# Where the gated values of a streaming encoder's MLP lie in SBUF: tiles of 6144 bytes in place of 5632, and halves that start 128 bytes past a multiple of 256

## The chip, the core and the metric

The kernel runs on one NeuronCore of a Trainium2 chip. The metric is the device time of one execution in microseconds; of several runs the median is taken. TensorE does the matrix products (PE in the profile, PEld its weight loads), VectorE (DVE) and ScalarE (ACT) the elementwise work, GpSimd (POOL) a little of it, and SyncE (SP) issues most DMAs.

## What is computed

One layer of a streaming encoder for 2048 prompt tokens and 64 sample tokens, in float32: a modulated RMSNorm, one input projection split between a pooling mixer and an mLSTM, an output projection with a gated residual, and then the part that the change touches, a gated MLP with a causal convolution of width 3:

```python
h2 = rmsnorm(x, g2) * (1 + sc2) + sh2
up = h2 @ w_up                                   # 1024 -> 2 * 2816
conv = b_conv + sum(w_conv[j] * upp[:, j:j + T] for j in range(3))
a, g = jnp.split(conv, 2, -1)
x = x + gt2 * ((jax.nn.silu(g) * a) @ w_down)    # 2816 -> 1024
```

A final RMSNorm follows. Every float32 operand of a product is split into a high and a low part (`float32r`), and the kernel multiplies high by high, high by low and low by high: three matmuls where the reference has one.

## The kernel before

The 2112 tokens of the MLP are worked on in three groups of 704 (`FT`), each group in two halves of 352 (`FH`). The 22 blocks of 128 hidden channels are cut into parts of 4 or 6 blocks (`PARTS`). Of a part, each block's up-projection is computed first (`Pair.products`, matmuls of line 1633). Their moving operands are the tiles `hx`, of 6144 bytes per partition. Each `hx` tile holds four runs of 352 values, 1536 bytes apart, and a run starts `HO` = 32 values (128 bytes) into its 1536 bytes.

After that come convolution, SiLU and gate, and the gated values are split into high and low parts in the tiles `av`. The down-projection reads these tiles as moving operands, in one of two ways:

- Parts of 4 blocks go through a seven-product scheme on halves of 352 (`quad_down`, matmuls of line 2125). There are nine such parts, each with 168 matmuls: 24, then 12 of line 1633 between, then 144. The text calls such a part a quad. Its tiles are held by the class `Quad`: `put` names the half that a product needs, `both` a whole row of two halves. `wide_hi` and `wide_lo` (ACT line 1858, DVE line 1861) write two halves in one instruction; `hi` and `lo` (lines 1842 and 1845) write one.
- Parts of 6 blocks read whole rows, in pieces of 448 and 256 values (matmuls of line 2271). `split_hi` and `split_lo` write these.

An `av` tile is `[P, 2, FT]`: the high part of 704 values, then the low part, 5632 bytes with no room left. There are seven (`AVB`). They also hold the sums of the down-projection's weights while those are formed (`quad_sums`). In the built program all seven `av` tiles start 160 bytes past a multiple of 256. Since 704 values are 2816 bytes, eleven times 256, both parts of a first half start at 160, and a second half, 1408 bytes on, at 32 past a multiple of 256. All `hx` tiles start at a multiple of 256, so every one of their runs starts at 128. Every block of weights in the MLP (`wt`) starts at a multiple of 256. For comparison: the moving operands of the output projection before the MLP (`mx`, matmuls of line 496) start at multiples of 256 in the first three of its four token groups, with 512 columns, and at 128 past one in the fourth, with 256 and 320 columns in turn.

The streams of PE, ACT, DVE and POOL in the MLP are in the order in which the code is written (a manual schedule). SP issues the DMAs ahead of need.

`fscr` hands out scratch rows of 2816 bytes; of `rb` (the factor of the norm spread over all partitions) and `ssum` (the sum of squares) there is one tile each. The residual rows `x0` to `x7` stand in the same pool as `av`, on both sides of it, and share its offset of 160.

Of the kernel before, what the change touches and what calls it, by code (L numbers as in the profile page):

```python
# [9 lines left out]
F32 = mybir.dt.float32  # L10
F32R = mybir.dt.float32r
AF = mybir.ActivationFunctionType
# [4 lines left out]
P = 128  # L17
# [8 lines left out]
FT = 704  # L26
FH = FT // 2
# [3 lines left out]
AVB = 7  # L31
# [16 lines left out]
HX, HO = 2 * 384, 32  # L48
# [19 lines left out]
def tile_layer(ctx: ExitStack, tc: tile.TileContext, xT, vecs, cst, rst, w_mod, w_ada, w_qkou, w_v, w_pool,  # L68
               w_out, w_up, w_down, w_quad, st_C, st_pool, yT, yS, o_pool, o_C, o_m, o_conv):
    nc = tc.nc  # L70
    act, dve, pool, pe = nc.scalar, nc.vector, nc.gpsimd, nc.tensor
# [18 lines left out]
    def m2_ps():  # L90
        return bank("m2")
# [11 lines left out]
    def scr():  # L103
        return sp.tile([P, TMAX], F32, tag="scr", name="scr")
# [170 lines left out]
    for g in range(NG):  # L275
# [9 lines left out]
        for bi, (lo, hi) in enumerate(o.blks):  # L285
            for (a, b, s) in o.segs:
                l, h = max(lo, a), min(hi, b)
# [14 lines left out]
    def halves(key, src, n):  # L302

        out = []
        for c in (0, n // 2):
            w = n // 2
            new = (key, c) not in place_of
            kept = hl_kept[place_of.setdefault((key, c), len(place_of)), :, :, :w]
            out.append((src[:, c:c + w], w, OUT, kept) if new else (kept, w, WHOLE, None))
        return out  # L310
# [49 lines left out]
    for g in range(NFG):  # L360
        held = None
        late = []
        for (f0, f1_) in PARTS[g]:
# [13 lines left out]
            for i, (n, k) in enumerate(order):  # L377
                if i == f1_ - f0 - 2:
                    stream += late
                c = f0 + k // 4 * 4  # L380
# [223 lines left out]
    RF = cp.tile([P, 6], F32, tag="RF", name="RF")  # L604
# [27 lines left out]
    def outproj(o, mix, between, behind_heads=None):  # L632
# [5 lines left out]
        for rows in [(0, 1)] + [(n,) for n in range(2, KD)]:  # L638
            xs = nx
            Ws = [Row() for _ in rows]  # L640
            pss = [[mm_ps() for _ in o.blks] for _ in rows]
            if len(rows) == 1:
                gemm(pss[0], Ws[0], mix, o, order=order, ups=(4,))
            else:
                for W, ps in zip(Ws, pss):
                    gemm(ps, W, mix, o, ks=order[:6], order=order)
                quiet.clear()
                for W, ps in zip(Ws, pss):
                    gemm(ps, W, mix, o, ks=order[6:], order=order, late=1)
                    if behind_heads:  # L650
                        behind_heads()
                        behind_heads = None
            nx = [load_x(rows[-1] + 1, o)] if rows[-1] + 1 < KD else []
            if rows[0] == 0:
                between()
            for n, x, ps in zip(rows, xs, pss):
                for (bi, pa, pb, a, b, s) in o.pieces:
                    add = now.scalar_tensor_tensor(out=x[:, a:b], in0=ps[bi][:, pa:pb], scalar=gt1(n, s), in1=x[:, a:b],
                                                   op0=ALU.mult, op1=ALU.add)
                    if rows[0] == 0:  # L660
                        row_done.append(add)
                nc.sync.dma_start(out=x2d[n, :, o.t0:o.t0 + o.T], in_=x[:, :o.T])
            if rows[0] == 0 and o.last:
                ssum = fscr("ssum")
            for n, x in zip(rows, xs):
                sq_acc(ssum, x[:, :o.T], o.T, n == 0)
# [15 lines left out]

    def fscr(dt=F32):
        if dt in ("rb", "ssum"):
            return spare[0].tile([P, FT], F32, tag=dt, name=dt)
        return spare[0].tile([P, FT], dt, tag="fscr", name="fscr", bufs=4)


    spare = []
# [89 lines left out]
    def behind_rows(d):  # L779
# [3 lines left out]
                          reason="behind_rows")  # L783

    def sums_of(xs, put, slow=False, pin=lambda d: d):

        H = FH
# [80 lines left out]
    if True:  # L868
# [144 lines left out]
        h, pb, pr0 = [], [], []  # L1013
# [475 lines left out]
        for o in groups:  # L1489
# [16 lines left out]
            if o.g == 0:  # L1506
                t = scr()
# [13 lines left out]
            for hd in range(NH):  # L1521
# [4 lines left out]
                if o.g == 0 and hd == 0:  # L1526
                    xs = rows_of(groups[1])
                    t = scr()
# [32 lines left out]
            h = hn  # L1561
# [5 lines left out]
    f2 = fctx.enter_context(tc.tile_pool(name="f2", bufs=1, side="right"))  # L1567
# [115 lines left out]
    def quad_sums(ds, lead=7):  # L1683

        for d in ds:
            for c in (0, 256):
                t = f2.tile([P, 2, FT], F32R, tag="av", name="qs", bufs=AVB)
                w = t.bitcast(F32).rearrange("p a t -> p (a t)")[:, :1024].rearrange("p (i c) -> p i c", i=4)
                nc.sync.dma_start(out=w, in_=w_quad[d, :, :, c:c + 256])
                for _ in range(lead):  # L1690
                    yield
                a11, a12, a21, a22 = (w[:, i] for i in range(4))
                dve.tensor_tensor(out=a22, in0=a21, in1=a22, op=ALU.add)
                yield
                dve.tensor_tensor(out=a21, in0=a11, in1=a21, op=ALU.subtract)
                yield
                dve.tensor_tensor(out=a11, in0=a22, in1=a11, op=ALU.subtract)
                yield
                dve.tensor_tensor(out=a12, in0=a12, in1=a11, op=ALU.subtract)
                yield  # L1700
                yield
                nc.sync.dma_start(out=dsum[d, :, :, c:c + 256], in_=w)
                yield
                yield

    def half_tile(nm):
        return f1.tile([P, FH], F32, tag=nm, name=nm)

    class Quad:

# [4 lines left out]
        def put(self, nm, m, part):  # L1715
            key, at = {"B11": (("a", m), 0), "T1": (("a", m), 1), "B21": (("b", m), 0), "B22": (("b", m), 1),
                       "T2": (("c", m), 0), "T3": (("c", m), 1), "T4": ("d", m)}[nm]
            if key not in self.tiles:
                self.tiles[key] = f2.tile([P, 2, FT], F32R, tag="av", name="av", bufs=AVB)
            return self.tiles[key][:, part, at * FH:(at + 1) * FH]  # L1720

        def both(self, nm, m, part):
            self.put(nm, m, part)
            return self.tiles["b" if nm == "B21" else "c", m][:, part, :]

    class Pair:

# [9 lines left out]
        def products(self, old):  # L1737
# [22 lines left out]
            b3 = self.b3 = take()  # L1760
            product(b3, Bo, "T1", True)
            self.s5 = half_tile("s5")
            act.activation(self.s5, b3.t[:, :FH], AF.Copy)
            rest((old, Pair.scale_a), (older, Pair.step_3))
# [90 lines left out]
            return self.quad.gated[self.m, i]  # L1855

        def wide_hi(self, nm, t):
            act.activation(self.quad.both(nm, self.m, 0), t[:, :FT], AF.Copy)

        def wide_lo(self, nm, t):  # L1860
            dve.tensor_tensor(out=self.quad.both(nm, self.m, 1), in0=t[:, :FT],
                              in1=self.quad.both(nm, self.m, 0).bitcast(F32), op=ALU.subtract)

        def step_2(self):
# [42 lines left out]
                self.lo("T4", self.blocks()[2])  # L1907

        def split_hi(self):
            self.d = self.d or f2.tile([P, 2, FT], F32R, tag="av", name="av", bufs=AVB)  # L1910
            for (a, b, s) in self.o.segs:
                act.activation(self.d[:, 0, a:b], self.tg[:, a + 2 * s:b + 2 * s], AF.Copy)
            self.av[self.i] = self.d
# [32 lines left out]
    def final(o, x3, ssum, squares):  # L1946
# [11 lines left out]
        yield  # L1958
        box = []
        yield from bcast_cols(RF, 0, FT, box, fscr)  # L1960
        yield
        yield
# [21 lines left out]
    def final_end(o, x3, sums, lo, hi):  # L1984
# [3 lines left out]
        for _ in range(YA if lo == 0 else 0):  # L1988
            yield
        ps = m2_ps()  # L1990
        rs = f2.tile([P, 5], F32, tag="rs", name="rs", bufs=1) if lo > 0 else RF
        if lo > 0:
            dve.memset(ps[:, :len(tiles)], 0.0)
            yield
# [59 lines left out]
        for (a, b) in YG:  # L2054
            if a % 2 == 0 or b - a == 2:
                t = f1.tile([P, 2, HX], F32R, tag="hx", name="y", bufs=2 * len(BN)).bitcast(F32).rearrange(
                    "p a t -> p (a t)")[:, :3 * w].rearrange("p (k t) -> p k t", t=w)
# [146 lines left out]
    for o in fgroups:  # L2204
        Bo = B[o.g]
        held = None
        for pi, part in enumerate(PARTS[o.g]):
# [4 lines left out]
            av = [None] * nf  # L2212
# [6 lines left out]
            for f in range(f0, f1_):  # L2219
                old, pair = pair, Pair(o, Bo, f, f - f0, av, quad)  # L2220
                pair.products(old)
                if o.g == 0 and f == 2:
                    bg[0].append(quad_sums(SUMS[0]))
                    bg[1].append(prepare(fgroups[1], fscr))
                if o.g == 0 and len(x3) < KD or pi == 0 and not bg[0]:
                    x3 += load_x2(o, range(len(x3), min(len(x3) + 2, KD)))
                if held is not None and nf > 2:
                    quad_down(o, held, pair, old)
                    held = None
                    if o.g == 0:  # L2230
                        bg[0].append(quad_sums(SUMS[1], 11))
                        bg[1].extend(aside)
# [94 lines left out]
            for secs in [(c,) for c in ENDS] if ends else (ENDS,):  # L2327
                sums = [(ssum, 0)]
                for n in range(NE, KD):
                    ps = [take() for _ in secs]  # L2330
                    down(ps, rows[n], range(nf), secs, ends)
                    if ends and n == KD - 1:
                        if secs[0][0] > 0:
                            drain(0)
                        bg[0].append(final_end(o, x3, sums, *secs[0]))
                        if secs[0][0] > 0:
                            tick(0)
                    down_end(n, ps, secs)
# [98 lines left out]
```

## Time and profile before

| | before |
|---|---|
| three runs | 2158.36, 2160.7, 2164.97 us (median 2160.7) |
| profiled execution: its time, its span | 2162.09 us, 2160.3 us |
| PE busy | 2142.7 us, 99% |
| DVE, ACT, POOL busy | 1650.1, 1101.7, 253.8 us |
| DMA moved | 541.09 MB, mean 250 GB/s |
| matmuls on `hx` (line 1633), on `av` halves (line 2125), on `av` rows (line 2271) | 5544, 1512, 1440 |

A matmul's recorded duration is longer than the distance to the next one's start, since matmuls overlap. In a row of the timeline, a start, a duration and a count stand side by side; the pace is the duration less that of the last matmul, over the count less one.

### The profile page before, as it was taken

The page shows a single profiled execution, that of the slowest core. Times are in us where ns is not written, and L with a number is a line of the kernel's source. Part 1 is how long each engine was busy: PE and PEld are TensorE (multiplying, and loading weights), DVE is VectorE, ACT ScalarE, POOL GpSimd, SP SyncE. Part 2 cuts the span into 40 slices and gives each one's busy share as a digit, 9 for nine tenths or more (in the row PEclk, how much of TensorE's full clock was granted, in tenths as well). Part 3 has the DMA queues.
Part 4 walks back from the last instruction along what each step waited for, and adds up shares of the span by engine and source line. Part 5 has one row for each costly group of instructions (what it writes and reads, how often), then busy time and mean ns, then how long its engine had stood idle before and what let it go on. Part 6 is the DMA issues. An engine that isn't in the chain of part 4 may idle for free.

```text
span 2160.3 us, 38129 instructions
## 1 busy us (share of the span) xinstructions
PE 2142.7 (99%) x13556; PEld 2038.7 (94%) x13556; DVE 1650.1 (76%) x3060; ACT 1101.7 (51%) x2192; POOL 253.8 (12%) x470
## 2 busy tenths in 40 slices
PE   8999999999999999999999999999999999999998
PEld 7888888888899999999999999999999999999998
DVE  5777768678675779788688668988886597887875
ACT  4554335234323557465556445655655364564554
POOL 0010000001000301010001110100101221121112
PEclk9999999999999999999999999999999999999999
DMA  8987997898799588797669986665668675455442
GB/s 321 326 315 237 317 324 246 282 320 274 243 298 302 196 280 307 252 336 246 233 219 314 329 299 207 235 214 205 228 222 273 218 261 182 171 180 183 172 169 85
DMA packets 296839, 541.09 MB, mean 250 GB/s; under 512 B 25760, under 2 KB 112800, under 8 KB 296648
## 3 DMA queue, kind: packets, MB, share of 16 engines
q1 hardware_dynamic: 286600, 514.13, 69.9%
q10 hardware_dynamic: 10048, 24.51, 2.9%
q8 instruction: 107, 1.75, 0.3%
q14 instruction: 84, 0.69, 0.1%
HBM read 412.56 MB, written 125.98 MB: 249 GB/s over the span
## 4 chain that ended last, share of the span: by engine, by line
PE 89%; DVE 5%; DMA 3%; issue 1%; ACT 1%; SPq 0%; POOL 0%; DVEq 0%; ACTq 0%; POOLq 0%
PE mm L1633 35%; PE mm L496 24%; PE mm L2271 10%; PE mm L2125 10%; PE mm L1171 3%; DVE wt L432 1%; DMA wt<-wsum 1%; PE m L1361 1%; PE m L1383 1%; PE m L1381 1%; PE m L1346 1%; DMA w<-w_ada 1%; DVE x L2094 1%; DVE tg L1611 1%; ACT tg L1606 0%
## 5 line engine op out<-in xcount | busy, mean ns | idle before, releaser
L1633 PE MATMUL mm<-hx,wt 128*128 128x352 f32 x5544 | 888.8, 321 | 2.2 <-DVE wt L432 1.3
L1633 PEld LDWEIGHTS mm<-hx,wt 128*128 128x128 f32 x5544 | 881.0, 188 | 4.5 <-DVE wt L432 3.2
L496 PE MATMUL mm<-hl,wt 128*128 128x512 f32 (+2 forms) x1920 | 385.3, 356 | 0.0
L432 DVE TENSOR_TENSOR wt<-raw,wt 128x512 fp32r<-128x512 f32 (+1 forms) x460 | 310.4, 681 | 75.0 <-ACT wt L429 74.9
L496 PEld LDWEIGHTS mm<-hl,wt 128*128 128x128 f32 x1920 | 314.8, 188 | 46.8 <-issue 3.6
L429 ACT ACTIVATE wt<-raw 128x512 fp32r<-128x512 f32 (+1 forms) x460 | 274.1, 603 | 163.3 <-PE mm L496 53.9
L2125 PE MATMUL mm<-av,wt 128*128 128x352 f32 x1512 | 247.4, 323 | 1.4 <-DVE x L2094 0.7
L2125 PEld LDWEIGHTS mm<-av,wt 128*128 128x128 f32 x1512 | 242.3, 188 | 4.0 <-DVE wt L432 2.0
L2271 PE MATMUL mm<-av,wt 128*128 128x448 f32 (+1 forms) x1440 | 231.3, 322 | 0.0
L2271 PEld LDWEIGHTS mm<-av,wt 128*128 128x128 f32 x1440 | 220.9, 188 | 9.7
L2094 DVE SCALAR_TENSOR_TENSOR x<-mm,MOD,x 128x352 f32<-128x352 f32 (+3 forms) x368 | 171.7, 507 | 73.3 <-PE mm L2271 58.3
L1681 ACT ACTIVATE mm<-mm 128x352 f32<-128x352 f32 x204 | 91.4, 448 | 240.9 <-PE mm L1633 177.1
L496 PE MATMUL mm<-mx,wt 128*128 128x512 f32 (+1 forms) x960 | 182.6, 352 | 0.0
L496 PEld LDWEIGHTS mm<-mx,wt 128*128 128x128 f32 x960 | 159.3, 188 | 22.5
L1611 DVE SCALAR_TENSOR_TENSOR ta<-ea,V,ta 128x704 f32<-128x704 f32 (+1 forms) x132 | 125.7, 952 | 61.3 <-ACT ta L1606 56.8
L1611 DVE SCALAR_TENSOR_TENSOR tg<-eg,V,tg 128x704 f32<-128x704 f32 (+1 forms) x132 | 125.7, 952 | 52.7 <-ACT tg L1606 50.2
L432 DVE TENSOR_TENSOR wt<-wt 128x512 fp32r<-128x512 f32 x204 | 138.8, 684 | 12.7 <-ACT wt L429 10.6
L429 ACT ACTIVATE wt<-wt 128x512 fp32r<-128x512 f32 x204 | 123.6, 621 | 31.3 <-DMA wt<-wsum 30.5
L1589 POOL COPY ea<-UC 128x2 f32<-128x2 f32 x66 | 34.7, 525 | 539.3 <-DVE ta L1611 425.3
L1829 ACT ACTIVATE tg<-tg 128x704 f32<-128x704 f32 (+1 forms) x66 | 52.5, 795 | 71.1 <-DVE tg L1611 71.1
L1171 PE MATMUL mm<-wt,hl 128*128 128x256 f32 (+1 forms) x576 | 71.2, 284 | 0.0
L1171 PEld LDWEIGHTS mm<-wt,hl 128*128 128x128 f32 x576 | 70.2, 189 | 0.8 <-issue 0.6
(315 smaller groups left out, 2204.4 us busy)
## 6 DMA issues: line engine op xcount, KB each, us to landing
wt<-wsplit SPq DMA_DIRECT2D x132, 512.0 KB, 4.3
raw<-w_up SPq DMA_DIRECT2D x198, 256.0 KB, 4.1
wt<-hl_kept SPq DMA_DIRECT2D x96, 512.0 KB, 6.0
wt<-wsum SPq DMA_DIRECT2D x132, 256.0 KB, 4.9
wsplit<-wt SPq DMA_DIRECT2D x66, 512.0 KB, 5.0
w<-w_up SPq DMA_DIRECT2D x88, 256.0 KB, 4.6
wsum<-w SPq DMA_DIRECT2D x44, 512.0 KB, 5.4
Bd<-fscr ACTq DMA_DIRECT2D x56, 352.0 KB, 3.9
```

The lines of the kernel that those rows point to most:

```text
L429: act.activation(u.w[:, 0, :u.n], u.raw[:, :u.n], AF.Copy)
L432: dve.tensor_tensor(out=u.w[:, 1, :u.n], in0=u.raw[:, :u.n], in1=u.w[:, 0, :u.n].bitcast(F32), op=ALU.subtract)
L496: pe.matmul(ps[bi][:, :hi - lo], U[:, a, k % 4 * P:(k % 4 + 1) * P], mv[k][:, b, lo:hi], start=(at == 0 and pi == 0), stop=(k == order[-1] ...
L1171: pe.matmul(ps[ti][:n, :cols], h[4 * kh + k4][:, b, lo:lo + n], U[:, a, k4 % 2 * cols:(k4 % 2 + 1) * cols], start=(kh == 0 and k4 == 0 and ...
L1589: pool.tensor_copy(ext[:, 0:2], UC[:, f, :])
L1611: dve.scalar_tensor_tensor(out=t[:, :E], in0=ext[:, j:j + E], scalar=wc(j, f), in1=t[:, :E], op0=ALU.mult, op1=ALU.add)
L1633: pe.matmul(bk.t[:, :FH], U[:, a, kc * P:(kc + 1) * P], Bo.at(nm, kc, b), start=(first and kc == 0 and pi == 0), stop=(kc == 3 and pi == 2 ...
L1681: act.activation(to.t[:, :FH], bk.t[:, :FH], AF.Copy)
L1829: act.activation(self.tg[:, :E], self.tg[:, :E], AF.Silu)
L2094: dve.scalar_tensor_tensor(out=x3[n][:, a:b], in0=bk.t[:, a - lo:b - lo], scalar=gt2(n, s), in1=x3[n][:, a:b], op0=ALU.mult, op1=ALU.add)
L2125: pe.matmul(bk.t[:, :FH], U[:, a, c:c + P], quad.put(op, m, b), start=(first and m == 0 and pi == 0), stop=(m == 1 and pi == 2), skip_grou ...
L2271: pe.matmul(bks[i].t[:, :hi - lo], U[:, a, k % 4 * P:(k % 4 + 1) * P], av[k][:, b, lo:hi], start=(k == 0 and (a, b) == PASSES[0]), stop=(k ...
```

## The change

An `av` tile becomes `[P, 2, HX]` with `HX` = 768: 6144 bytes, the high and the low part 3072 bytes apart. For a quad, each part is cut into two slots of 1536 bytes with a half of 352 values at the start of each. Whole rows are taken from the eighth value on (32 bytes in), without a gap between the halves. `wide_hi` and `wide_lo` now write two runs of 352 with a gap of 128 bytes in place of one run of 704; `halves` gives the source the same shape.

To make room, `ssum` takes the one tile that `rb` has, by having the same tag; 2816 bytes are freed. The tag of the small tile `rs` gets a second buffer of 32 bytes, of which nothing is written; the pool is laid out against the end of the memory, and its other tiles move by that much. In the built program all `av` tiles then start 128 past a multiple of 256: all halves, of both parts, are at 128, and whole rows are at 160 as before. `x0` to `x7` go from 160 to 128, `rb` from 128 to 0.

```diff
     def fscr(dt=F32):
         if dt in ("rb", "ssum"):
-            return spare[0].tile([P, FT], F32, tag=dt, name=dt)
+            return spare[0].tile([P, FT], F32, tag="rb", name=dt)
...
-                t = f2.tile([P, 2, FT], F32R, tag="av", name="qs", bufs=AVB)
+                t = gated("qs")
...
+    def gated(name="av"):
+        return f2.tile([P, 2, HX], F32R, tag="av", name=name, bufs=AVB)
+
+    def halves(t):
+        return t[:, :FT].rearrange("p (h t) -> p h t", h=2)
...
             if key not in self.tiles:
-                self.tiles[key] = f2.tile([P, 2, FT], F32R, tag="av", name="av", bufs=AVB)
-            return self.tiles[key][:, part, at * FH:(at + 1) * FH]
+                self.tiles[key] = gated().rearrange("p a (h t) -> p a h t", h=2)[:, :, :, :FH]
+            return self.tiles[key][:, part, at]
...
         def wide_hi(self, nm, t):
-            act.activation(self.quad.both(nm, self.m, 0), t[:, :FT], AF.Copy)
+            act.activation(self.quad.both(nm, self.m, 0), halves(t), AF.Copy)
 
         def wide_lo(self, nm, t):
-            dve.tensor_tensor(out=self.quad.both(nm, self.m, 1), in0=t[:, :FT],
+            dve.tensor_tensor(out=self.quad.both(nm, self.m, 1), in0=halves(t),
                               in1=self.quad.both(nm, self.m, 0).bitcast(F32), op=ALU.subtract)
...
-            self.d = self.d or f2.tile([P, 2, FT], F32R, tag="av", name="av", bufs=AVB)
+            self.d = self.d or gated()[:, :, 8:8 + FT]
...
-        rs = f2.tile([P, 5], F32, tag="rs", name="rs", bufs=1) if lo > 0 else RF
+        rs = f2.tile([P, 5], F32, tag="rs", name="rs", bufs=2) if lo > 0 else RF
```

No instruction is added, removed or moved: on every engine and queue the built programs have the same instructions in the same order, and each waits for the same semaphore values. What differs are addresses and, in 36 ACT and 36 DVE instructions, the shape (2 runs of 352 in place of 704).

More of the change, by code (lines that the diff above doesn't have):

```diff
@@ L1718, in put @@
             if key not in self.tiles:
-                self.tiles[key] = f2.tile([P, 2, FT], F32R, tag="av", name="av", bufs=AVB)
-            return self.tiles[key][:, part, at * FH:(at + 1) * FH]
+                self.tiles[key] = gated().rearrange("p a (h t) -> p a h t", h=2)[:, :, :, :FH]
+            return self.tiles[key][:, part, at]
         def both(self, nm, m, part):
             self.put(nm, m, part)
-            return self.tiles["b" if nm == "B21" else "c", m][:, part, :]
+            return self.tiles["b" if nm == "B21" else "c", m][:, part]
     class Pair:
```

## The prediction

> **What bounds the kernel.** I read the page first, for the engine that sets the time, then the timeline of PE alone, for the pace of each kind of matmul, and last what DVE does in the nine quads.
>
> ```profile
> span 2160.3 us, 38129 instructions
> PE 2142.7 (99%) x13556; PEld 2038.7 (94%) x13556; DVE 1650.1 (76%) x3060; ACT 1101.7 (51%) x2192; POOL 253.8 (12%) x470
> ...
> PE 89%; DVE 5%; DMA 3%; issue 1%; ACT 1%; SPq 0%; POOL 0%; DVEq 0%; ACTq 0%; POOLq 0%
> ...
> L1633 PE MATMUL mm<-hx,wt 128*128 128x352 f32 x5544 | 888.8, 321 | 2.2 <-DVE wt L432 1.3
> ...
> L2125 PE MATMUL mm<-av,wt 128*128 128x352 f32 x1512 | 247.4, 323 | 1.4 <-DVE x L2094 0.7
> ...
> L2271 PE MATMUL mm<-av,wt 128*128 128x448 f32 (+1 forms) x1440 | 231.3, 322 | 0.0
> ```
>
> PE is busy for 99% of the span and carries 89% of the chain that ended last. A change that adds and removes no instruction can gain only by the pace of matmuls, or by the few microseconds in which PE waits. The mean durations (321, 323, 322 ns) don't show the pace, because matmuls overlap. The timeline does; its columns are start, duration, engine, line, operation, count:
>
> ```profile
> 1107.87 23.21 PE L2125 MATMUL mm<-av,wt 128*128 128x352 f32 x144
> 1130.92 12.10 PE L1633 MATMUL mm<-hx,wt 128*128 128x352 f32 x74
> ...
> 1344.88 51.47 PE L1633 MATMUL mm<-hx,wt 128*128 128x352 f32 x324
> 1396.18 4.01 PE L2125 MATMUL mm<-av,wt 128*128 128x352 f32 x24
> ...
> 1658.48 42.15 PE L2271 MATMUL mm<-av,wt 128*128 128x448 f32 x264
> ```
>
> Both kinds of line 1633 and 2125 stream 352 columns against 128 by 128 weights, three passes per block. On `hx` a matmul starts every (51.47 - 0.32) / 323 = 158.36 ns; on the halves in `av` every (23.21 - 0.32) / 143 = 160.07 ns. From start to start it is the same: 1107.87 to 1130.92 is 23.05 us for 144, and 1344.88 to 1396.18 is 51.30 for 324. The difference is 1.71 ns per matmul. The runs in `hx` begin 128 bytes past a multiple of 256 and end on one; the halves in `av` begin at 160 or 32. After the change they begin and end as those in `hx` do.
>
> **The change part by part.**
>
> *Halves at 128.* If start and end set the pace, 1512 matmuls gain 1.71 ns: 2.59 us at most. Not all of it reaches the end, since two of the nine quads run at DVE's pace:
>
> ```profile
> 1482.61 8.97 PE L2125 MATMUL mm<-av,wt 128*128 128x352 f32 x54
> 1492.31 14.69 PE L2125 MATMUL mm<-av,wt 128*128 128x352 f32 x90 [0.74 <-DVE x L2094]
> ...
> 1563.89 1.45 PE L2125 MATMUL mm<-av,wt 128*128 128x352 f32 x8
> 1565.88 22.40 PE L2125 MATMUL mm<-av,wt 128*128 128x352 f32 x136 [0.53 <-DVE wt L432]
> ```
> ```profile
> core 0: us, DVE busy (x), PEclk, DMA share, GB/s
> 1107.90:1130.90 23.00, 20.04 (x38) 1.00 0.52 172
> ...
> 1482.70:1506.80 24.10, 21.98 (x42) 1.00 0.52 179
> 1563.90:1588.00 24.10, 22.50 (x44) 1.00 0.52 175
> 1773.50:1796.60 23.10, 21.23 (x52) 1.00 0.53 178
> ```
>
> In the second and third window PE stops for 0.74 and 0.53 us until DVE has added to the residual or split weights, and these quads take 24.1 us where the others take 23.0 to 23.2. What is late there is DVE, and a faster PE waits longer for it. I count their 2 x 168 matmuls as no gain (336 x 1.71 = 0.57 us). The gain then lies between 2.59 us, if these two gain too, and 2.02. I take **2.0 us**: in both the stop comes after some of the 144 matmuls, so at least what these gain is lost, and DVE is busy for over 91% of the whole of both.
>
> *Whole rows.* They start at 160 as before, and their pace, (42.15 - 0.32) / 263 = 159.05 ns over pieces of 448 and 256 columns, stays. What does change for them is the distance of low from high part, 2816 to 3072 bytes. In `hx` that distance is 1536. No row of this trace has 3072. The nearest is that 158.36 on one side and the present 159.05 on the other, so I take 0; the end below is the same 1.71 ns for 1440 matmuls, 2.5 us, the end above nothing, since no row shows a slower pace for such pieces than the present one.
>
> *Two runs in place of one (wide copies).* Here is the cost of the present instructions, and of two that write one run and four runs of 512 values:
>
> ```profile
> L1861 DVE TENSOR_TENSOR av<-tg,av 128x704 fp32r<-128x704 f32 x36 | 31.9, 885 | 0.1
> L1845 DVE TENSOR_TENSOR av<-tg,av 128x352 fp32r<-128x352 f32 x54 | 28.2, 522 | 12.1 <-ACT av L1842 12.0
> L432 DVE TENSOR_TENSOR wt<-wt 128x512 fp32r<-128x512 f32 x204 | 138.8, 684 | 12.7 <-ACT wt L429 10.6 <-DMA yT<-x 2.0
> L268 DVE TENSOR_TENSOR nd<-nd,sf 128x512 f32<-128x512 f32 x16 | 11.1, 692 | 15.1 <-POOL sf L1404 15.1
> ```
> ```profile
> L1858 ACT ACTIVATE av<-tg 128x704 fp32r<-128x704 f32 x36 | 28.2, 784 | 9.4 <-DVE tg L1837 9.3
> L1842 ACT ACTIVATE av<-tg 128x352 fp32r<-128x352 f32 x54 | 26.5, 490 | 16.4 <-DVE tg L1837 10.3 <-DVE tg L1849 6.1
> ```
>
> `nd` is written as four runs of 128 with a gap between, at 692 ns against 684 for one run: 8 ns for three more runs. So 885 becomes some 888 ns, and 36 of them cost DVE 0.1 us, which lies beside PE's work but for the two quads at DVE's pace (8 of 36: 0.02 us). The upper end is that a two-run instruction costs as much as two of one run: 2 x 522 - 885 = 159 ns on DVE and 2 x 490 - 784 = 196 ns on ACT. The lower end is 0. I take 0, by the row of `nd`, which is the one with gaps.
>
> *One tile for `rb` and `ssum`.* A shared tile can bring a wait of the one's writer for the other's last reader. The built programs wait for the same values at the same places, so there is none: 0 from both sides. The extra 32 bytes of `rs` cost nothing but address space.
>
> *Residual rows and `qs` at 128 in place of 160.* DVE reads and writes them, DMAs fill and empty them. DVE's 368 additions of line 2094 now work on halves at 160 or 32, afterwards at 128 or 0. The fills of `x` take a median of 5.8 us, those of `fscr`, whose rows start on multiples of 256, 4.8 us for the same size:
>
> ```profile
> x<-x2d SPq DMA_DIRECT2D x24, 352.0 KB, 5.8
> ...
> fscr<-x2d SPq DMA_DIRECT2D x16, 352.0 KB, 4.8
> ```
>
> Should the 1 us be the offset's, it is still hidden: the rows are loaded while the products run, and no wait of PE in this trace is for `x` from a DMA. Its cover is the 50 us of products ahead of each quad (the row of 324). I take 0; from below at most the two stops of 0.74 and 0.53 us could go, if DVE's part in them became quicker.
>
> The sum against the profiled execution: span 2160.3 - 2.0 = 2158.3 us, its time 2162.09 - 2.0 = 2160.1. That execution lies 1.4 us over the median of the three runs (2160.7), so I predict 2160.7 - 2.0 = **2158.7 us** for the median, -0.09%. A change within 0.3% (6.5 us) is about what this kernel's measurement can't tell from none.
>
> **The rivals.**
>
> *The offset is not what sets the pace: 2160.7 us.* For it speaks another tile at 128:
>
> ```profile
> 344.84 43.72 PE L496 MATMUL mm<-mx,wt 128*128 128x512 f32 x192
> 732.12 51.36 PE L496 MATMUL mm<-mx,wt 128*128 128x256 f32 x384
> ```
>
> The first row has 512 columns from multiples of 256, at (43.72 - 0.39) / 191 = 226.9 ns. The second has 256 and 320 columns in turn (288 in the mean), all from 128, at (51.36 - 0.31) / 383 = 133.3 ns. From 512 columns to the 352 of the halves it is 66.8 ns for 160 columns, 0.418 per column; from these to 288 it is 26.8 ns for 64, 0.418 too. So `mx` at 128 lies on the line of the tiles at 0, 32 and 160, and only `hx` lies 1.7 ns below it. Against the rival: these pieces of `mx` also end at 128, while those of `hx` end on a multiple of 256, as the new halves will; and 352 columns at two different offsets, 160 and 32, have one pace. The Trainium skill, page "SBUF — State Buffer", section "Door 1: The DMA port swizzle", speaks for this rival: SBUF has lines of 16 bytes, and an access pays where it crosses into a new line with too few hits in the last. 0, 32, 128 and 160 all begin such a line and every run is contiguous, so by that rule all these paces would lie on one line, and the halves would gain nothing: 2160.7 us. The trace disagrees for `hx` (158.36 against 160.07) and agrees for `mx`.
>
> *Whole rows gain as well: 2156.2 us.* If the parts' distance (a multiple of 512 bytes in `hx` and in the new tiles, not in the old ones, nor in `mx`, whose parts lie 2304 apart) is what counts, 1440 matmuls gain 1.71 ns too, 2.5 us more. For it speaks that `mx` is then explained; beyond that no row speaks for or against it, and it needs a second rule beside the one of the forecast.
>
> *Slower: the wide copies at the price of two instructions, 2171.5 us.* In a quad, `wide_hi` and `wide_lo` stand right ahead of the products that read them. At their upper ends 36 pairs cost 36 x (0.159 + 0.196) = 12.8 us, and with all of that on PE's path it would be 2158.7 + 12.8. To be slower by over 6.5 us it needs 8.5 us on the path, 0.24 us for each pair. Against it: 8 ns for three more runs in `nd`, and PE's rows of 144 without a stop in the quads outside of DVE's pace, so ACT and DVE have room.
>
> **How the numbers follow.** Halves alone gain: 0.60, 2158.7. No gain: 0.23, 2160.7. Rows gain as well: 0.09, 2156.2. Copies slower: 0.04, up to 2171.5. The other 0.04 is for a moved stop, either way. Three runs of one kernel spread over 6.6 us, so the range adds some 4 us to either side of the first and second: 2154.5 to 2163.5, which leaves out the copies, the lower part of the third case's spread, and the farther of the moved stops. Faster by over 0.3% needs 4.5 us beyond the forecast, rows and a vanished stop together or spread: 0.07. Slower by over 0.3%: 0.05, the copies mostly. Within: 0.88.
>
> **What would show it.** Right: rows of 144 of line 2125 at 22.8 us for 144 starts in place of 23.05, `hx` and the rows of 264 unchanged, wide copies at 780 to 790 and 885 to 890 ns, the quads at DVE's pace still near 24 us. Wrong: rows of 144 still at 23.05 (the first rival); rows of 264 under 41.5 us (the second); wide copies over 950 ns with PE stopping for `av` (the third). I would also be wrong if a stop of PE of over 2 us appeared at another place, since DVE's order against PE's shifts by the gain.

## The result and the profile after

| | before | changed |
|---|---|---|
| median of 16 runs each | 2160.73 us | 2178.12 us |
| lowest, highest | 2157.83, 2167.48 us | 2158.07, 2184.13 us |
| profiled execution: its time, its span | 2162.09, 2160.3 us | 2161.37, 2159.6 us |

The ratio over all runs is 1.0066, 95% interval 1.0052 to 1.0081 (that of the two medians alone is 1.0080): slower by under 1%, clear of the noise, and outside of the predicted range. The runs of the changed kernel are spread in an unusual way. Three of 16 lie between 2158.07 and 2162.07 us, the other 13 between 2172.01 and 2184.13. The profiled execution is one of the three short ones, so its page looks as if the forecast had come true. First the page, then PE's timeline (start, duration, engine, line, operation, count) at a whole quad and at a whole row:

```profile
span 2159.6 us, 38129 instructions
PE 2142.5 (99%) x13556; PEld 2037.2 (94%) x13556; DVE 1649.8 (76%) x3060; ACT 1104.0 (51%) x2192; POOL 256.2 (12%) x470
...
L1633 PE MATMUL mm<-hx,wt 128*128 128x352 f32 x5544 | 890.7, 322 | 0.7 <-DVE wt L432 0.6
...
L2131 PE MATMUL mm<-av,wt 128*128 128x352 f32 x1512 | 245.5, 322 | 2.1 <-DVE x L2100 0.7
```
```profile
1111.80 22.96 PE L2131 MATMUL mm<-av,wt 128*128 128x352 f32 x144
1134.60 5.71 PE L1633 MATMUL mm<-hx,wt 128*128 128x352 f32 x35
...
1506.27 51.46 PE L1633 MATMUL mm<-hx,wt 128*128 128x352 f32 x324
...
1657.75 42.15 PE L2277 MATMUL mm<-av,wt 128*128 128x448 f32 x264
```

The halves take 1134.60 - 1111.80 = 22.80 us for 144 starts, 158.33 ns each, as forecast; whole rows are unchanged at 42.15 us for 264. But two rows do not fit, one of them in the trace of the kernel before:

```profile
1143.31 55.93 PE L1633 MATMUL mm<-hx,wt 128*128 128x352 f32 x334 [0.29 <-DVE wt L432]
```
```profile
937.95 55.93 PE L1633 MATMUL mm<-hx,wt 128*128 128x352 f32 x334 [0.27 <-DVE wt L432]
```

The first is of before, the second of the changed kernel. Here a matmul starts every (55.93 - 0.33) / 333 = 167.0 ns, with the same operands' shapes and offsets as in the row of 324, where it is (51.46 - 0.32) / 323 = 158.33. The granted clock is 1.00 in both. So a stream of these matmuls has two paces, and the prediction read only one. A longer execution of the changed kernel (2171.49 us, from the tenth run below) shows what that is worth; its page, its timeline and a window, then the same window of the short execution:

```profile
span 2169.7 us, 38129 instructions
...
L1633 PE MATMUL mm<-hx,wt 128*128 128x352 f32 x5544 | 897.2, 323 | 0.7 <-DVE wt L432 0.6
...
L2131 PE MATMUL mm<-av,wt 128*128 128x352 f32 x1512 | 249.8, 324 | 1.8 <-DVE x L2100 0.7
```
```profile
1767.60 24.40 PE L2131 MATMUL mm<-av,wt 128*128 128x352 f32 x144
1791.84 54.16 PE L1633 MATMUL mm<-hx,wt 128*128 128x352 f32 x324
1845.84 4.16 PE L2131 MATMUL mm<-av,wt 128*128 128x352 f32 x24
1849.84 2.16 PE L1633 MATMUL mm<-hx,wt 128*128 128x352 f32 x12
1851.84 24.16 PE L2131 MATMUL mm<-av,wt 128*128 128x352 f32 x144
1875.84 54.16 PE L1633 MATMUL mm<-hx,wt 128*128 128x352 f32 x324
...
2043.84 68.16 PE L1633 MATMUL mm<-hx,wt 128*128 128x352 f32 x408
2111.84 3.45 PE L2277 MATMUL mm<-av,wt 128*128 128x448 f32 x20
```
```profile
1800.00:2100.00 300.00, 300.00 (x1801) 1.00 0.52 172
```
```profile
1800.00:2100.00 300.00, 299.79 (x1889) 1.00 0.53 176
```

From 1770 to 2110 us every row has one pace, from start to start (1845.84 - 1791.84) / 324 = 166.67 ns, products and halves alike: 2055 matmuls in one piece. In the windows (PE's busy time, its matmuls, its clock) PE is busy all the time in both; in one it starts 1801 matmuls, in the other 1889. Busy time and granted clock show nothing of it. Only a count over a stretch, or a row's duration over its count, does.

### The profile page after: what moved, and what is told of

Read it like the earlier page. It is cut to its first block, busy times and chain, and to the rows that moved or that the text cites. A ratio compares the mean times of both kernels' runs of the same rounds, so it can differ in the third digit from the quotient of the medians.

```text
span 2159.6 us, 38129 instructions
## 1 busy us (share of the span) xinstructions
PE 2142.5 (99%) x13556; PEld 2037.2 (94%) x13556; DVE 1649.8 (76%) x3060; ACT 1104.0 (51%) x2192; POOL 256.2 (12%) x470
## 4 chain that ended last, share of the span: by engine, by line
PE 88%; DVE 5%; DMA 4%; issue 2%; ACT 1%; SPq 0%; POOL 0%; DVEq 0%; POOLq 0%; ACTq 0%
PE mm L1633 36%; PE mm L496 23%; PE mm L2277 10%; PE mm L2131 9%; PE mm L1171 3%; DVE wt L432 1%; DVE x L2100 1%; PE m L1361 1%; PE m L1383 1%; DMA hl_kept<-wt 1%; PE m L1381 1%; PE m L1346 1%; DMA mx<-xT 1%; DMA wt<-wsum 1%; DVE tg L1611 0%
```

## The experiments

The theory: at 128 a stream of 352-column matmuls has two paces, 158.33 and 166.67 ns, and keeps the one that it starts in until something ends it (**L**, two paces). Its rivals: the shared tile or the moved rows bring a new wait (**W**), and the new place of the halves is slow by itself (**P**).

**The changed kernel once more, and its parts.** Four kernels, measured together. The first is the changed kernel again, run once:

> The changed kernel once more, for a trace of one of its long executions: 13 of its 16 runs took 2172 to 2184 us, and the one profiled was not among them (2161.4). Theory A (the quicker quads let DVE fall behind, and PE waits): the 17 us stand as idle time of PE, in or next to the quads, matmuls of line 2131 at 158.3 ns. Theory B (an address slows an engine or a DMA in most executions): the pace of a group of instructions or the landing time of a group of DMAs is different from the trace of the short execution, by 17 us in all, and it has to be one whose tile moved: halves (12 ns each over 1512), rows (12 ns over 1440), or x and qs. Theory C (nothing of this kernel, a state of the chip): the loss is spread over all stages, the attention ahead of the MLP too, which has no changed address.

It took 2164.62 us. Its timeline:

```profile
1313.22 4.16 PE L2131 MATMUL mm<-av,wt 128*128 128x352 f32 x24
...
1319.22 24.16 PE L2131 MATMUL mm<-av,wt 128*128 128x352 f32 x144
1343.22 54.16 PE L1633 MATMUL mm<-hx,wt 128*128 128x352 f32 x324
...
1427.22 54.16 PE L1633 MATMUL mm<-hx,wt 128*128 128x352 f32 x324
```

The quad of 144 takes 24.0 us from start to start, where that of the short execution took 22.80, and the slow pace runs on through products, quad and products: 1092 matmuls in one piece. The longest slow piece in before is the one of 334. None of the three theories of this run holds as it stands. Against A: quads run at 166.67 ns, and PE's stops in the streams of 352 columns add up to 5.8 us, less than the 7.6 of the short execution. Against B, which wanted a group whose tile moved: the products on `hx` are slow too, and their runs lie at 128 as before. Against C: from the first matmul to the first of line 1633 it takes 777.2 us in this trace, 777.7 in the short one and 777.5 in that of before.

The second moves the halves by 8 values, to 160, and leaves all else:

```diff
-... .rearrange("p a (h t) -> p a h t", h=2)[:, :, :, :FH]
+... .rearrange("p a (h t) -> p a h t", h=2)[:, :, :, 8:8 + FH]
```

> The changed kernel with each half 8 values later in its slot (160 past a multiple of 256, as the first halves before), all else as in the change. Theory A (the quicker pace of the halves upsets a wait): halves at 160.0 ns, time back to 2160 to 2162 us in all runs. Theory B (placement of x, qs, rb or the rows): still 2172 to 2184 in most runs. Theory C (state of the chip): as the kernel before in the same call or slower with it.

2165.38 us (2158.92 to 2169.47), ratio 1.0021 [1.0011, 1.0032]. That is neither A's 2160 to 2162 us in all runs nor B's 2172 to 2184. It spreads over 10.6 us where the changed kernel spreads over 26, and its highest run lies 2.5 us below the group of 13. So most of the loss hangs on the halves' place, not on the tiles' size or on the shared tile.

The third is before with only the shared tag for `rb` and `ssum`:

```diff
-            return spare[0].tile([P, FT], F32, tag=dt, name=dt)
+            return spare[0].tile([P, FT], F32, tag="rb", name=dt)
```

> The kernel before with one part of the change alone: the sum of squares in the spread factor's tile; no other address moves. Theory A: 2160 to 2162 us. Theory B, if the shared tile or rb at 0 is what costs: over 2170 in most runs; if it is x or av: 2160 to 2162.

2161.21 us, ratio 1.0002 [0.9993, 1.0012]: the sharing costs nothing, and W falls for it. The fourth is before with only the second buffer of `rs`, which moves `av`, `x` and `qs` to 128 and the halves to 128 and 0:

```diff
-        rs = f2.tile([P, 5], F32, tag="rs", name="rs", bufs=1) if lo > 0 else RF
+        rs = f2.tile([P, 5], F32, tag="rs", name="rs", bufs=2) if lo > 0 else RF
```

> The kernel before with the 32 bytes of rs alone: av, qs and x move from 160 to 128 past a multiple of 256, halves from 160 and 32 to 128 and 0, rows from 160 to 128. Theory A: first halves (half of 1512) at 158.3 to 160 ns, so 2158 to 2161 us, or long runs if any quickening upsets a wait. Theory B, if x or qs at 128 is what costs: over 2170 us in most runs.

2164.52 us, ratio 1.0018 [1.0008, 1.0027]. No run is over 2169 us, so W falls for `x` and `qs` as well, though A's 2158 to 2161 us is missed too. Its whole rows start at 128, and they alone explain most of it:

```profile
1657.57 42.68 PE L2271 MATMUL mm<-av,wt 128*128 128x448 f32 x264
```

That is (42.68 - 0.32) / 263 = 161.06 ns against 159.05 from 160, 2.0 ns for 1440 matmuls or 2.9 us.

**Can the pace be taken away, or cut?** Three kernels and a scan, measured together. The changed kernel again, for another long execution:

> The changed kernel a third time, for its spread on this chip and for one more trace. Theory L (lock): a stream of 352-column matmuls from 128 past a multiple of 256 has two steady paces, 158.3 and 166.7 ns, and keeps the one that it starts in until PE stops or a matmul from another offset comes between. In the changed kernel products and quads are one stream, so the slow pace can hold over several quads. The time is then 2156 us plus 8.33 ns for each matmul at 166.7: 2161 for 600, 2166 for 1200, 2178 for 2600. Rival W (waits): the time over 2160 is idle time of PE, and the pace is 158.3 ns throughout.

2171.80, 2183.51 and 2164.83 us; the profiled one (the first) had a slow piece of 1044 matmuls at its end. It has 2040 slow matmuls in all, for which the sum of L gives 2173 us; 2171.80 were measured. Next, 18 extra matmuls in the changed kernel, at the start of each quad and ahead of the first product behind it, of 64 columns; their result is overwritten by the matmul that follows:

```diff
         if first:
             bk.start(FH)
+            if cut:
+                cut.pop()
+                pe.matmul(bk.t[:, :64], ones_r, ones_r[:, :64], start=True, stop=True)
...
+                    if not count:
+                        pe.matmul(bk.t[:, :64], ones_r, ones_r[:, :64], start=True, stop=True)
```

> The changed kernel with 18 small matmuls more (64 columns of ones, from another offset, overwritten by what follows), one at the start of each quad and one at the first product after it. Theory L: the slow pace can't cross these places, so a stretch at 166.7 ns has at most some 400 matmuls, as in the kernel before; the runs come back to 2157 to 2166 us, median about 2161, none over 2172. If one small matmul doesn't end the slow pace, as the change itself. Rival W: 18 matmuls more change no wait, and most runs stay at 2172 to 2184.

2168.49 us (2166.14 to 2170.60), ratio 1.0034 [1.0021, 1.0047]. The right half: no slow piece is longer than the 408 of the products between two of the extra matmuls, and no run is over 2171 us. At one quad:

```profile
1508.13 0.19 PE L1634 MATMUL mm<-ones_r 128*128 128x64 f32 x1
1508.16 54.23 PE L1637 MATMUL mm<-hx,wt 128*128 128x352 f32 x324
1562.23 0.19 PE L2133 MATMUL mm<-ones_r 128*128 128x64 f32 x1
1562.26 4.04 PE L2137 MATMUL mm<-av,wt 128*128 128x352 f32 x24
```

The slow 324 end at the extra matmul, and the 24 behind it are fast. The missed half is the median: some streams start slow right behind an extra matmul, as the 324 do here.

Then before with products' tiles at 32 in place of 128 (`HX, HO = 2 * 384, 8`):

> The kernel before with the runs of hx starting 32 bytes into their slots (HO = 8) in place of 128. Theory L: at 32 past a multiple of 256 there is one pace, 160.0 ns, as the old second halves show, and no slow stretches. Of 5544 matmuls those at 158.3 lose 1.67 ns (up to 9.2 us) and those at 166.7 (324 in the trace of before, 2.7 us) gain: 2166 to 2169 us, with less spread than the kernel before (its runs 2157.5 to 2164.8). Rival (what counts is the distance of the parts, not the start): 158.3 ns and 2160 us as before.

2165.18 us (2164.11 to 2166.67), ratio 1.0015 [1.0005, 1.0025], 0.8 us below the forecast. All of `hx` runs at one pace, (52.00 - 0.32) / 323 = 160.0 ns, and the runs spread over 2.6 us, where those of before, measured beside it, spread over 10.4:

```profile
1343.65 52.00 PE L1633 MATMUL mm<-hx,wt 128*128 128x352 f32 x324
```

So the second pace goes with the place 128, and with it most of the spread. P falls: 128 is at its first pace the quicker place (158.33), and the loss lies in the second. The scan gives each tile of products in before another start (`AT = dict(B11=0, T1=4, T2=8, B21=16, B22=24, T3=28, T4=32)`, in values of 4 bytes):

> The kernel before with another start for each of the seven operands of the up-projection: B11 at 0, T1 at 16, T2 at 32, B21 at 64, B22 at 96, T3 at 112 and T4 at 128 bytes past a multiple of 256, each read by 12 matmuls in a row. Theory L in its narrow form (only 128 has two paces): T4 alone at 158.3 or 166.7, the others at 160.0. In a wider form (what counts is whether start or end meets a boundary of 64 or 128 bytes): B11 and B21 as well. By the rule of 16-byte lines all seven have one pace, as all seven starts are multiples of 16.

2169.31 us, in one run. Mean distance of starts, worked out from the trace's records over pieces of twelve without a stop, 62 to 66 pieces each:

```
start past a multiple of 256 bytes    0      16     32     64     96     112    128
ns from start to start              161.2  160.0  160.3  160.1  162.6  161.6  158.8
```

At 128 it is 158.5 in most pieces and 166.0 and 166.1 in two. No other start is as quick, and in these short pieces none shows a second pace. The narrow form of L is half right: 128 alone has two paces, but 0, 96 and 112 are not at 160.0.

**What ends the slow pace?** `T4`, one operand of each quad, goes back to where it lay before the change (160 and 32), so that twelve matmuls of another place stand between the streams:

```diff
+                self.tiles[key] = (gated()[:, :, 8:8 + FT].rearrange(...) if nm == "T4" else
```

> The changed kernel, but with the operand T4, the last of each half of a quad, where it lay before (its first half at 160, its second at 32 past a multiple of 256, without a gap); the other six at 128 as in the change. So each quad has six matmuls from 160 and 32 in its middle and six more right ahead of the products that follow... for both row blocks, 24 of its 168. Theory L: the stream from 128 is cut at the end of each half of a quad, in the way in which the kernel before cut it, so no slow stretch is longer than some 500 matmuls, and starts after 32 seldom fall to the slow pace (none of 18 in the traces of before and of the kernel that only shares the tile). 1296 matmuls keep 158.3 ns, 2.2 us less half a microsecond: median 2157.5 to 2160.5, none over 2170. If starts after 32 fall to the slow pace as often as starts after a stop (15 of 148), 2162 to 2168. Rival W (waits): as the change, 2172 to 2184.

2185.87 us (2184.42 to 2189.41), ratio 1.0115 [1.0099, 1.0132]: missed by far, the slowest of all. The changed kernel beside it, the run from which the lines of the long execution are:

> The changed kernel in the same call, for comparison and one more trace. Theory L: 2158 to 2184 us with a median over 2168; in its trace, 2155 to 2156 us plus 8.33 ns for each matmul at 166.7 ns, within 2 us. Rival W: the time over 2160 is idle time of PE.

2182.06 us (2171.49 to 2186.35), ratio 1.0081 [1.0056, 1.0107]. Its highest run is 2 us over the forecast. Its trace has 2052 slow matmuls, so L gives 2172.1 to 2173.1 us; 2171.49 were measured, while the stops of PE in these streams went down (6.4 us against 7.6 in the short execution), so the rival W falls. Then I blamed the matmul that stands last before a stream, and took extra matmuls of 256 columns from 160, a place behind which no stream had started slow so far (0 of 40, behind whole rows), at the places of the first extra ones:

```diff
-                pe.matmul(bk.t[:, :64], ones_r, ones_r[:, :64], start=True, stop=True)
+                pe.matmul(bk.t[:, :256], ones_r, quad.raw[:, 0, 8:264], start=True, stop=True)
```

> The changed kernel with 18 other matmuls more, at the same places as the 18 of 64 columns: 256 columns from 160 past a multiple of 256, the form of the last piece of a whole row; what they write is overwritten. In ten traces so far none of 40 streams that began after such a piece took the slow pace, against 17 of 178 after a stop. Theory L with the way of entry set by the last matmul before: none of the 18 streams that begin behind the new matmuls is slow, slow stretches begin at stops alone and end within 324 matmuls; 18 x 0.12 = 2.1 us more than the fast form (2154 to 2156.5 us): median 2157 to 2161, none over 2168. Theory L with the way of entry set by a longer history (the six-matmul pieces of T4 let the slow pace through): streams begin slow there as after 64 columns, some one in six or more, and the median is 2164 us or more.

2183.88 us (2176.49 to 2188.55), ratio 1.0107 [1.0091, 1.0124]: missed again, so the last matmul before a stream doesn't set its pace. Its timeline shows what happens in its place:

```profile
1343.95 0.28 PE L1633 MATMUL mm<-av,ones_r 128*128 128x256 f32 x1
1344.07 54.15 PE L1636 MATMUL mm<-hx,wt 128*128 128x352 f32 x324
1398.06 0.28 PE L2135 MATMUL mm<-av,ones_r 128*128 128x256 f32 x1
1398.17 4.15 PE L2139 MATMUL mm<-av,wt 128*128 128x352 f32 x24
...
1404.17 24.16 PE L2139 MATMUL mm<-av,wt 128*128 128x352 f32 x144
1428.16 0.28 PE L1633 MATMUL mm<-av,ones_r 128*128 128x256 f32 x1
1428.28 54.15 PE L1636 MATMUL mm<-hx,wt 128*128 128x352 f32 x324
```

The slow pace is handed on over the extra matmul, 13 times out of 13 in this trace. The last run takes the same matmuls at the same places with 64 columns of the same tile, so that only the length differs:

> The changed kernel with the 18 extra matmuls of the run before (at the start of each quad and ahead of the first product after it, reading the quad's own tile at 160), 64 columns long in place of 256. The records of the two runs with extra matmuls differ in more than the length: 64 columns of the row of ones (at 224) ended the slow pace in 5 places of 5 where a slow stream ran into one, 256 columns of the quad's tile (at 160) in none of 13. Behind the 64 columns the second matmul starts some 247 ns after the first, so PE stands still for some 90 ns; behind the 256 columns nothing stands still (280 ns over both). Theory G (the short standstill ends the slow pace): the 64 columns of the quad's tile leave the same standstill and end it in every place, no slow stretch is longer than 408 matmuls, and the median is that of the run with ones, 2166 to 2171 us. Theory T (what is read, or its place, decides): the slow pace is passed on as by the 256 columns of the same tile, stretches of over 1000 matmuls stand in the trace, and the median is 2178 to 2188 us.

2163.66 us (2161.38 to 2167.32), ratio 1.0015 [1.0005, 1.0024], 20 us below the 256 columns:

```profile
1342.12 0.19 PE L1633 MATMUL mm<-av,ones_r 128*128 128x64 f32 x1
1342.14 54.23 PE L1636 MATMUL mm<-hx,wt 128*128 128x352 f32 x324
1396.22 0.19 PE L2135 MATMUL mm<-av,ones_r 128*128 128x64 f32 x1
1396.25 4.05 PE L2139 MATMUL mm<-av,wt 128*128 128x352 f32 x24
...
1402.03 22.96 PE L2139 MATMUL mm<-av,wt 128*128 128x352 f32 x144
```

The slow 324 end at the extra matmul; the quad behind it is fast. No slow piece is longer than 333. Both kinds cost the same: from the last matmul ahead of it to the first behind, 256 columns take 280 ns in place of 158, 122 more; with 64 columns the second one behind starts 435 ns after in place of 317, 118 more. So the 20 us are not their price. That the operand's place decides falls: place and tile were the same, and the length alone made the difference. That it is the standstill behind the short matmul which ends the slow pace fits, though the time was put too high; it was not tested apart from the length.

All traces together, counted in the records of twelve executions (all but the kernel with `hx` at 32 and the scan):

```
what stands between two streams at 128            slow before: ended, handed on   fast before: next slow, next fast
24 matmuls of whole rows, from 160                    18   0                          0   37
one extra matmul of 64 columns                         8   0                          4   22
one extra matmul of 256 columns                        0  13                          2    2
12 halves at 160 and 32 (T4 moved back)                1  11                          4    2
12 halves at 0                                         2   0                          0   16
24 or 144 halves at 160 and 32, as in before           1   0                          0   33
144 halves at 160                                      3   0                          1    5
a stop of PE, a start 225 ns or more after the last    4   2                         18  127
```

## Why the prediction was wrong

**The step that failed** is the term "Halves at 128: 1512 matmuls gain 1.71 ns". It took the pace at 128 as one number, read from a row of 324. The runs showed two, 158.33 and 166.67 ns, of which the second is 8.33 ns slower than the first and 6.67 slower than the 160.0 that the halves had. The table counts slow matmuls in blocks of twelve and takes off 8.33 ns for each, and 2.1 us for the 18 extra matmuls where there are any. Then it takes off PE's stops: each step of 225 ns or more between two 352-column matmuls of these lines, less 159 ns, without the step behind an extra matmul.

| execution | its time | slow matmuls | time without them | stops | time without both |
|---|---|---|---|---|---|
| before | 2162.09 | 324 | 2159.4 | 8.3 | 2151.1 |
| before, shared tile | 2159.43 | 240 | 2157.4 | 7.0 | 2150.4 |
| changed, halves at 160 | 2160.23 | 444 | 2156.5 | 6.3 | 2150.3 |
| changed, short | 2161.37 | 588 | 2156.5 | 7.6 | 2148.9 |
| changed, three others | 2164.62, 2171.80, 2171.49 | 1272, 2040, 2052 | 2154.0, 2154.8, 2154.4 | 5.8, 6.6, 6.4 | 2148.2, 2148.2, 2148.0 |
| changed, extra 64 columns (ones; quad's tile) | 2170.19, 2163.31 | 1548, 900 | 2155.2, 2153.7 | 7.1, 5.3 | 2148.1, 2148.4 |
| changed, extra 256 columns | 2185.72 | 4008 | 2150.2 | 2.5 | 2147.7 |
| changed, T4 moved back | 2184.42 | 3852 | 2152.3 | 3.6 | 2148.7 |

The times differ by 26 us. Without both, the eight executions with halves at 128 (in the last, all but those of T4) lie within 1.2 us of each other, and the three with halves at 160 or 32 some 2 us above them. So the gain of the faster halves is there and about as large as the term said (2.59 us at most). But the 2040 slow matmuls of the longest traced execution of the changed kernel cost 17.0 us, of which the fewer stops give some back. No execution of the changed kernel over 2172 us was traced. By the same sum a time of 2184 us would take some 3400 to 4000 slow matmuls (an estimate); the two last rows show that a kernel of this build gets to as many.

**A second misreading, a small one.** The prediction counted seven quads as free of DVE. From start to start, the 144 matmuls of the nine quads took 23.05, 23.06, 23.42, 24.23, 24.22 and four times 23.32 us in before, and 22.80, 22.85, 23.22, 24.32, 24.11, 23.22, 23.21, 23.22 and 23.20 in the short execution, where no half was slow. Only the first two gained most or all of the 0.25 us that 144 halves should. The last four stop for 0.27 us in before and for some 0.34 in the short execution, and gained 0.10 to 0.12. All 1512 halves together took 1.2 us less, where 2.0 were forecast. What the last four wait for is seen in the weight loads (PEld), which the forecast does not show: one line of before, then two of the short execution:

```profile
1774.81 3.35 PEld L2125 LDWEIGHTS mm<-av,wt 128*128 128x128 f32 x21 [0.29 <-DVE wt L432]
```
```profile
1854.21 0.69 DVE L432 TENSOR_TENSOR wt<-wt 128x512 fp32r<-128x512 f32 x1
...
1854.95 1.10 PEld L2131 LDWEIGHTS mm<-av,wt 128*128 128x128 f32 x7 [0.36 <-DVE wt L432]
```

DVE finishes the low part of a weight block at 1854.90 us, and the load of that block starts at 1854.95. A faster PE only waits longer there, as the prediction said of the two quads that it did see.

**Why more are slow after the change.** In before, halves at 160 and 32 stand between the streams of products. They have one pace, 160.0 ns, and no stream behind them was slow (0 of 34, of which one came behind a slow stream; 144 halves at 160 ended three more of three). In the changed kernel products and quads are one stream, so a start that happens to be slow lasts through several quads. The slow pace seems to protect itself, too. Two rows of the short execution at one of the last four quads:

```profile
1853.46 23.37 PE L2131 MATMUL mm<-av,wt 128*128 128x352 f32 x144
1876.66 51.46 PE L1633 MATMUL mm<-hx,wt 128*128 128x352 f32 x324
```

The 144 take 0.41 us more than the 22.96 of the whole quad above: this is the stop for DVE's weight block, some 1.1 us into each of these four quads, and the stream starts anew behind it. The execution of 2171.49 us has this stop in the first of the four alone (24.40 in place of 24.16); the stream that starts behind it is the slow one. From there on PE is late enough to stop no more (no weight load in these quads waits for DVE), and nothing ends the stream before the whole rows. The execution of 2171.80 us does the same two quads later: a stop in the first three, a slow stream behind the third, no stop in the fourth. That the slow pace keeps itself up in this way is read from these two traces; no run tests it.

**Right** were: the fast pace of the halves (22.80 us for 144); the two quads at DVE's pace, still at 24.32 and 24.11 us; whole rows at 42.15 us for 264, so the rival of rows that gain falls; `rb` and `ssum` in one tile at 0; residual rows and `qs` at 128 with no new wait of PE for them; and the wide copies, forecast at 780 to 790 and 885 to 890 ns:

```profile
L1867 DVE TENSOR_TENSOR av<-tg,av 128x704 fp32r<-128x704 f32 x36 | 32.0, 888 | 0.1
```
```profile
L1864 ACT ACTIVATE av<-tg 128x704 fp32r<-128x704 f32 x36 | 28.3, 785 | 8.6 <-DVE tg L1843 8.4
```

So the rival of slow copies falls as well. That the short execution lies within the predicted range is luck: 588 of its matmuls were slow, and nothing in the runs holds the number there. The rival that the offset does not set the pace falls by the run with `hx` at 32 (158.33 to 160.0). The rule that the Trainium skill has in "SBUF — State Buffer", section "Door 1: The DMA port swizzle", would give all starts of the scan one pace, since each is a multiple of 16 bytes; the trace disagrees, with 158.8 to 162.6 ns.

**The range** came from the spread of three runs of before, which was itself for the most part the two paces: with `hx` at 32, ten runs spread over 2.6 us. None of the rivals held a second pace, and the row that shows it (334 matmuls, 55.93 us) stood in the trace of before, next to the one of 74 that I quoted.

**Open** is what decides the pace at a start: 18 of 145 streams started slow behind a stop and a fast stream, with nothing in the records to tell them apart. Open too is why the two kinds of extra 64 columns differ by some 5 us in the median, why the halves at 160 stay 0.2% above before, and why 24 matmuls of whole rows end the slow pace without a standstill (18 of 18) where twelve halves do not, or why a stop of PE ends it only 4 times of 6. No version that was run is faster than before.

## What to carry to other kernels

Before a pace is taken as a price, work it out for every long row of the timeline, not for one, and look for a second value at full clock: here the spread between executions was for the most part such a second value. Read the weight loads for waits as well as the matmuls. An operand at an offset that is slower by 1% may be what ends a bad pace (here four slow streams of four), so a change that makes all operands alike can lengthen what was short before. And where runs of one kernel fall into two groups, one profiled execution says little until it is known to which group it belongs.

## What the runs showed of the hardware

- 352-column matmuls with a weight load each, at a granted clock of 1.00, have two steady paces when the moving operand starts at 128 past a multiple of 256 bytes: 158.33 and 166.67 ns, kept for as many as 2055 matmuls.
- At starts of 32 and 160 the pace is 160.0 ns in long rows. In pieces of twelve, 16, 32 and 64 have 160.0 to 160.3 ns, and 0, 96 and 112 have 161.2, 162.6 and 161.6. Pieces of 448 and 256 columns prefer another start: 159.05 ns in the mean from 160, 161.06 from 128.
- One extra matmul of 64 columns ended the slow pace 8 times of 8, one of 256 columns 0 times of 13, though both cost 0.12 us.
